# Gate and up projections of a hybrid block with the activations stationary and a few block products saved

## The chip, the cores and the metric

One core of one Trainium2 chip runs the whole kernel. The metric is the device time of one execution in microseconds (us); 0.2% of it, about 2.3 us, is the smallest difference spoken of here as a change.

## The reference

The kernel computes one block of a streaming encoder for 256 tokens of width 2048, all in fp32:

```python
h = rmsnorm(x, norm1_gain)
proj = h @ w_in                                  # attention and recurrence inputs
mixed = concat([attention(proj), recurrence(proj)])
x = x + mixed @ w_out
h2 = rmsnorm(x, norm2_gain)
ff = silu(h2 @ w_gate) * (h2 @ w_up)             # 2048 -> 5632, the part that is changed
x = x + ff @ w_down                              # 5632 -> 2048
out = rmsnorm(x, final_gain)
```

## The kernel before

Each fp32 operand of a large product is split into a high part in fp32r (ScalarE, line 86) and a low part, the difference (VectorE, line 87). A product is then three: high x high, high x low, low x high. Weights come from memory in loads of 1 MB (`load_chunk`, three buffers "raw"), all on SyncE's queue, and are split into pairs of tiles `wh` and `wl` of 1024 elements per partition, four buffers each. The eight banks of the accumulator memory are two pools of four: `pacc` ("acc") for the main sums and `paux` ("aux") for everything else.

The program has four stages. The input projection with attention and recurrence woven in comes first (to about 326 us). The `w_out` stage (to 436 us) has the activations stationary: `nat_step` (lines 142 to 144) loads 128 tokens of `ma` or `mr` as the stationary operand and streams 512 columns of `wh` or `wl`. As its columns come out they are added to `x2`, and `second_split` turns `x2` with four transposes at a time (`pair_transpose`, line 313), scales it by `norm2_gain` and splits it into `h2`, which holds the high and low parts, k-tile by k-tile, with tokens as columns.

The gate and up stage (lines 656 to 666) loops over 22 blocks of 256 columns; in each, gate and then up run through `tr_product` (lines 158 to 172). Here the weights are stationary: a tile of 128 columns of `wh` meets the high and low halves of `h2` in one product of 512 columns (line 167), and the same tile of `wl` meets the high half in one of 256 (line 169). The result comes out with the features in the partitions, which is what the down projection wants. `tr_evac` (lines 174 to 179) adds the two halves and multiplies by `R2`, a row of token scales that `row_rstd` makes by two small products (line 255); then come silu, the product, and the split into `fh` and `fl`.

The down stage works in two groups of 1024 output columns. For each pair of k-tiles a step is either plain (24 products of 512 columns, four banks c00, c01, c10, c11 by token half and column half) or fast: seven block products in place of eight, with sums of activation blocks (`row_sums`, kept in `sf`) and of weight blocks (lines 737 to 739), into c00, c01, c10 and four side banks m1, m5, m6, m7. After the last fast pair `spread` adds the side banks to `x2` (lines 774 to 782). Plain and fast pairs alternate; 7 of 22 pairs are fast in the first group and 8 in the second. The groups' last pairs run bank by bank, so that the banks are emptied one after another (`run_blocks`).

The order of the program is not the order of the engines: a list scheduler of the framework orders each engine's instructions from the dependencies, the pools' buffers and its own estimate, and each engine then works through its line in that order, waiting where it must.

Of the kernel before, what the change touches and what calls it, by code (L numbers as in the profile page):

```python
# [8 lines left out]
F32 = mybir.dt.float32  # L9
# [7 lines left out]
P = 128  # L17
# [10 lines left out]
KP = KF // 2  # L28
FAST = 8
BANKS = ("c00", "c01", "c10", "c11", "m1", "m5", "m6", "m7")  # L30
# [13 lines left out]
def hybrid_block(ctx: ExitStack, tc: tile.TileContext, x, xT, w_in, w_out, w_gu, w_down,  # L44
# [574 lines left out]
    R2 = const.tile([P, S], F32, name="R2")  # L619
    rst2 = [None]  # L620

    def second_rstd():
        s2 = small.tile([P, NT], F32, tag="ssum", name="ssum")
        nc.vector.tensor_reduce(s2, ss2, AX.X, ALU.add)
        rst2[0] = rstd_of(s2, NT, float(D), "r2")

    def second_rows():
        row_rstd(R2, rst2[0])

# [19 lines left out]
    queue.append(lambda: [f() for f in both_splits] and second_rstd())  # L649
    queue.append(second_rows)  # L650
# [5 lines left out]
    gup = tc.tile_pool(name="gup", bufs=1)  # L656
    gu = gup.__enter__()
# [8 lines left out]
    gup.__exit__(None, None, None)  # L666

    dn = ctx.enter_context(tc.tile_pool(name="dn", bufs=1))
    sf = act_t.tile([P, 2, FAST // 2, 4, 2, P], F32R, tag="hx", name="sf")
    fg = dn.tile([P, D], F32, name="fg")

    def row_sums(i):
        k4 = slice(4 * i, 4 * i + 4)
        a = dn.tile([P, 2, 2, S], F32, tag="ta", name="a")
        sm = dn.tile([P, 4, 2, P], F32, tag="tb", name="sm")
        nc.vector.tensor_tensor(a, fh[:, k4, :].rearrange("p (j k) t -> p j k t", k=2).bitcast(F32),
                                fl[:, k4, :].rearrange("p (j k) t -> p j k t", k=2).bitcast(F32), ALU.add)  # L680
# [5 lines left out]
        split(sf[:, 0, i], sf[:, 1, i], sm)  # L686

    def load_fg():
        dma(fg, fgain.to_broadcast([P, D]))
        nc.scalar.activation(warm, fg[:, 0:1], AF.Square)  # L690
        nc.scalar.activation(warm, warm, AF.Sqrt)
# [8 lines left out]
    def load_pair(g, j):  # L700
        return load_chunk(w_down, g * KP + j).rearrange("p (b n) -> p b n", n=W)

    def f_of(k, t):
        tok = slice(t * P, (t + 1) * P)
        return fh[:, k, tok], fl[:, k, tok]

    def s_of(j, i):
        return sf[:, 0, j // 2, i, j % 2, :], sf[:, 1, j // 2, i, j % 2, :]

    class Group:  # L710
        def __init__(self, g, items):
            self.g, self.items = g, items
            self.bank = {}
            ns = sum(1 for kind, _ in items if kind == "s")
            nd = len(items) - ns
            self.left = {n: 3 * (ns + 2 * nd) if n in ("c00", "c01", "c10") else
                         6 * nd if n == "c11" else 3 * ns for n in BANKS}
            self.total = dict(self.left)

        def open(self):  # L720
            for n in BANKS:
                pool, tag = (pacc, "acc") if n[0] == "c" else (paux, "aux")
                self.bank[n] = pool.tile([P, W], F32, tag=tag, name=n)

        def mul(self, n, lhs, rhs):
            if not self.bank:
                self.open()
# [5 lines left out]
        def fast(self, j):  # L733
            raw = load_pair(self.g, j)
# [9 lines left out]
            return [("m1", f_of(2 * j, 0), b11), ("m5", s_of(j, 0), t1), ("m7", s_of(j, 2), t3),  # L744
                    ("c01", s_of(j, 3), b22), ("c00", f_of(2 * j + 1, 0), b21),
                    ("m6", s_of(j, 1), t2), ("c10", f_of(2 * j + 1, 1), t4_)]

        def plain(self, j):
            raw = load_pair(self.g, j)
            steps = []  # L750
            for k in range(2):
                parts = halves_of(raw[:, 2 * k:2 * k + 2])
                steps += [(f"c{t}{h}", f_of(2 * j + k, t), parts[h if k == 0 else 1 - h])
                          for t in range(NT) for h in range(2)]
            return steps
# [5 lines left out]
        def run_blocks(self, steps, blocks, after):  # L761
            for t, h in blocks:
                self.run([st for st in steps if st[0] == f"c{t}{h}"])
                after(t, h)

# [18 lines left out]
    def add_res(gr, t, h):  # L784
        cols = gr.cols(h)
        nc.vector.tensor_tensor(x2[:, t, cols], gr.bank[f"c{t}{h}"], x2[:, t, cols], ALU.add)
        jk = dn.tile([P, W], F32, tag="jk", name="jk")
        slot = 2 * gr.g + h
        nc.scalar.activation(jk, x2[:, t, cols], AF.Square, accum_out=ss3[:, t, slot:slot + 1])

    def gained(gr, t, h):
        cols = gr.cols(h)
        nc.vector.tensor_tensor(x2[:, t, cols], x2[:, t, cols], fg[:, cols], ALU.mult)

    def finish(ps, t):
# [7 lines left out]
        jk = dn.tile([P, 2, S], F32, tag="jk", name="jk")  # L803
# [14 lines left out]
        nc.vector.scalar_tensor_tensor(x2[:, t, c0:D], x2[:, t, c0:D], r, fg[:, c0:D], ALU.mult, ALU.mult)  # L818
# [4 lines left out]
    def order_of(fast, lead):  # L823
        slow = [j for j in range(KP) if j not in fast]
        items = [("d", j) for j in slow[:lead]]
        mid = slow[lead:-2]
        for n, j in enumerate(fast):
            items += [("s", j)] + [("d", k) for k in mid[n:n + 1]]
        return items + [("d", k) for k in mid[len(fast):]] + [("d", j) for j in slow[-2:]]

    groups = [Group(0, order_of(list(range(FAST - 1)), 6))]
    todo = [(0, kind, j) for kind, j in groups[0].items]
    second = order_of(list(range(FAST)), 1)
    todo += [(1, kind, j) for kind, j in second]
    sums = list(range(FAST // 2))
    n_fast, held = [0, 0], []

    def prepare(g, kind, j):
        if g == len(groups):
            groups.append(Group(1, second))  # L840
        return groups[g].fast(j) if kind == "s" else groups[g].plain(j)

    def last_block(t, h):
        if h == 0:
            add_res(groups[1], t, h)
            gained(groups[1], t, h)
        else:
            finish(groups[1].bank[f"c{t}{h}"], t)

    edge = len(groups[0].items) - 1  # L850
    steps = prepare(*todo[0])
    for n, (g, kind, j) in enumerate(todo):
        if n == edge:
            now, steps = steps, prepare(*todo[n + 1])
            order = ((0, 0), (0, 1), (1, 0), (1, 1))
            groups[0].run_blocks(now, order, lambda t, h: add_res(groups[0], t, h))
            for t, h in order:
                gained(groups[0], t, h)
            continue
        if n < len(todo) - 2:  # L860
            groups[g].run(steps)
        else:
            held += steps
        if kind == "s":
            n_fast[g] += 1
            if n_fast[g] == sum(1 for k, _ in groups[g].items if k == "s"):
                groups[g].spread()
        if sums and n >= 1:
            row_sums(sums.pop(0))
        if n == 5:  # L870
            load_fg()
        if n + 1 < len(todo):
            steps = prepare(*todo[n + 1])
    groups[1].run_blocks(held, ((0, 0), (0, 1), (1, 0), (1, 1)), last_block)
# [8 lines left out]
def _pairs(w, c0):  # L883
    b = w[:, c0:c0 + 2 * W].reshape(KP, 2, P, 2, W)
    return [b[:, 0, :, 0], b[:, 0, :, 1], b[:, 1, :, 1], b[:, 1, :, 0]]
# [48 lines left out]
```

## Time and profile before

| | us |
|---|---|
| median of three runs (lowest, highest) | 1167.95 (1167.85, 1169.08) |
| the profiled execution | 1168.06 |
| its span, first to last instruction | 1166.2 |
| gate and up stage, in the span | 436 to 926 |
| down stage | 926 to 1152 |

The span is the part of the execution that the trace covers. PE is TensorE's products, PEld its loads of stationary operands, DVE is VectorE, ACT ScalarE. Products are pipelined: the trace gives one of 512 columns some 0.39 us from start to end, while the next one starts 0.23 us after it. So PE's pace is read from start to start, and a result is there at the end.

### The profile page before, as it was taken

Reading aid. Unit: us, or ns where it says so; the run is one execution under the profiler, and the core shown is the slowest. Engines: PE = TensorE matmul, PEld = TensorE weight load, DVE = VectorE, ACT = ScalarE, POOL = GpSimd, SP = SyncE. Lnnn points to the kernel's source line nnn. Section 1 sums busy time; section 2 is a strip of 40 time slices with the busy share of each in tenths; the row PEclk is TensorE's granted clock in tenths of the full one; section 3 lists DMA queues with packets and bytes.
Section 4 is the critical chain, followed back from the end, with each engine's and each line's share of the span. In section 5 each row is a group of like instructions: output and inputs, shape, how many; then the busy total and the mean of one; then the engine's idle time right before and its main releaser. Section 6 shows DMA issues by size and latency. Waiting matters only on the chain.

```text
span 1166.2 us, 15524 instructions
## 1 busy us (share of the span) xinstructions
PE 1154.1 (99%) x6121; PEld 989.3 (85%) x6121; DVE 815.2 (70%) x1092; ACT 624.0 (54%) x856; POOL 19.0 (2%) x33
## 2 busy tenths in 40 slices
PE   9999999999999999999999999999999999999996
PEld 7888888888888888888888888888888887888885
DVE  7577768947746556666666666666666698898885
ACT  7565556747554445444444454444454555555553
POOL 3300000000000000000000000000000000000000
PEclk9999999999999999999999999999999999999999
DMA  8655444554744555555555555555455546556561
GB/s 314 242 207 192 148 173 163 204 177 151 262 171 162 187 187 182 184 184 193 200 182 183 194 200 182 183 198 198 180 186 196 196 181 217 204 192 217 211 222 73
DMA packets 35065, 223.85 MB, mean 192 GB/s; under 512 B 4145, under 2 KB 4657, under 8 KB 9521
## 3 DMA queue, kind: packets, MB, share of 16 engines
q1 hardware_dynamic: 34992, 222.87, 54.3%
q8 instruction: 48, 0.79, 0.3%
q14 instruction: 25, 0.20, 0.1%
HBM read 220.75 MB, written 2.10 MB: 191 GB/s over the span
## 4 chain that ended last, share of the span: by engine, by line
PE 96%; DMA 1%; DVE 1%; ACT 1%; SPq 0%; issue 0%; ACTq 0%; DVEq 0%
PE acc L167 38%; PE acc L169 19%; PE c L729 15%; PE acc L142 5%; PE acc L144 5%; PE acc L143 5%; PE m L729 3%; PE vps L143 1%; PE vps L144 1%; PE vps L142 1%; DMA raw<-in_w_down_dram 1%; DMA raw<-in_w_in_dram 0%; DVE wl L87 0%; SPq L83 0%; PE pa L531 0%; PE po L550 0%
## 5 line engine op out<-in xcount | busy, mean ns | idle before, releaser
L87 DVE TENSOR_TENSOR wl<-raw,wh 128x1024 fp32r<-128x1024 f32 (+1 forms) x418 | 493.3, 1185 | 276.4 <-ACT wh L86 271.7
L86 ACT ACTIVATE wh<-raw 128x1024 fp32r<-128x1024 f32 (+1 forms) x418 | 426.2, 1023 | 367.7 <-PE acc L167 215.6
L167 PE MATMUL acc<-h,wh 128*128 128x512 f32 x1408 | 488.6, 394 | 0.0
L169 PE MATMUL acc<-h,wl 128*128 128x256 f32 x1408 | 390.9, 278 | 0.0
L167 PEld LDWEIGHTS acc<-h,wh 128*128 128x128 f32 x1408 | 264.8, 188 | 60.9
L169 PEld LDWEIGHTS acc<-h,wl 128*128 128x128 f32 x1408 | 264.4, 188 | 0.0
L167 PE MATMUL acc<-hx,wh 128*128 128x512 f32 x512 | 179.7, 395 | 0.0
L169 PE MATMUL acc<-hx,wl 128*128 128x256 f32 x512 | 143.2, 280 | 0.0
L167 PEld LDWEIGHTS acc<-hx,wh 128*128 128x128 f32 x512 | 96.2, 188 | 21.3
L729 PE MATMUL c<-wl,fh 128*128 128x512 f32 x262 | 102.2, 390 | 0.0
L729 PE MATMUL c<-wh,fh 128*128 128x512 f32 x262 | 102.0, 391 | 0.2 <-ACT wh L86 0.2
L729 PE MATMUL c<-wh,fl 128*128 128x512 f32 x262 | 102.1, 390 | 0.0
L169 PEld LDWEIGHTS acc<-hx,wl 128*128 128x128 f32 x512 | 96.7, 189 | 0.1
L177 ACT COPY tb<-acc 128x256 f32<-128x256 f32 x120 | 43.3, 364 | 78.5 <-PE acc L169 78.5
L178 DVE TENSOR_TENSOR tb<-acc,tb 128x256 f32<-128x256 f32 x120 | 50.1, 420 | 30.3 <-ACT tb L177 30.3
L729 PEld LDWEIGHTS c<-wh,fh 128*128 128x128 f32 x262 | 49.1, 188 | 11.2 <-ACT wh L86 0.6
L729 PEld LDWEIGHTS c<-wl,fh 128*128 128x128 f32 x262 | 49.2, 188 | 10.5 <-DVE wl L87 0.3
L729 PEld LDWEIGHTS c<-wh,fl 128*128 128x128 f32 x262 | 49.2, 188 | 10.1
L142 PE MATMUL acc<-wh,hx 128*128 128x512 f32 x128 | 50.5, 394 | 0.0
L144 PE MATMUL acc<-wh,hx 128*128 128x512 f32 x128 | 50.0, 390 | 0.0
L143 PE MATMUL acc<-wl,hx 128*128 128x512 f32 x128 | 49.9, 390 | 0.0
L729 PE MATMUL m<-wh,sf 128*128 128x512 f32 x90 | 32.8, 391 | 0.1
(254 smaller groups left out, 1121.6 us busy)
## 6 DMA issues: line engine op xcount, KB each, us to landing
raw<-in_w_gu_dram SPq DMA_DIRECT2D x88, 1024.0 KB, 4.8
raw<-in_w_in_dram SPq DMA_DIRECT2D x48, 1024.0 KB, 4.8
raw<-in_w_down_dram SPq DMA_DIRECT2D x44, 1024.0 KB, 4.8
raw<-in_w_out_dram SPq DMA_DIRECT2D x16, 1024.0 KB, 4.8
raw<-in_w_in_dram SPq DMA_DIRECT2D x12, 512.0 KB, 7.1
raw<-in_w_in_dram SPq DMA_DIRECT2D x8, 256.0 KB, 4.8
x<-in_x_dram SPq DMA_DIRECT2D x2, 1024.0 KB, 9.7
out_dram<-x SPq DMA_DIRECT2D x8, 256.0 KB, 2.6
```

The lines of the kernel that those rows point to most:

```text
L86: nc.scalar.activation(hi, src, AF.Copy)
L87: nc.vector.tensor_tensor(lo, src, hi.bitcast(F32), ALU.subtract)
L142: nc.tensor.matmul(ps[t], lhsT=xh[:, tok], rhs=wh, start=kt == 0, stop=False)
L143: nc.tensor.matmul(ps[t], lhsT=xh[:, tok], rhs=wl, start=False, stop=False)
L144: nc.tensor.matmul(ps[t], lhsT=xl[:, tok], rhs=wh, start=False, stop=kt == kts - 1)
L167: nc.tensor.matmul(ps[m].rearrange("p j t -> p (j t)"), lhsT=wh[:, col], rhs=both, start=kt == 0, stop=False)
L169: nc.tensor.matmul(ps[m][:, 0, :], lhsT=wl[:, col], rhs=rhs[:, kt, 0, :], start=False, stop=kt == KD - 1)
L177: nc.scalar.copy(tb, ps[m][:, 1, :])
L178: nc.vector.tensor_tensor(tb, ps[m][:, 0, :], tb, ALU.add)
L729: nc.tensor.matmul(self.bank[n], lhsT=a, rhs=b, start=self.left[n] == self.total[n], stop=self.left[n] == 1)
```

## The change

Gate and up now run in the manner of the down stage. A group is 512 gate columns beside the 512 up columns that belong to them, so there are eleven groups of eight k-tile pairs. The weights are stored in pairs of k-tiles by blocks (`_pairs`), the activations `h2` are stationary, and the weights stream by 512 columns. The class `Group` serves both projections: `Gated` and `Down` are its two kinds, and `run_groups` runs all pairs of all groups in line, with the next pair prepared behind the one that runs. The first gated group has plain pairs only; in the ten others pairs 0 and 1 are fast, in the order plain 2, fast 0, plain 3, fast 1, plain 4 to 7. `hs` holds the sums of the activation blocks of those two pairs and is made once.

The result of a group has tokens in the partitions, `ff` with one half of the tokens beside the other. The scale of a token is now one number per partition (`rst2`), applied inside silu and inside the last multiplication; `R2` and its two small products are gone. `ff_split` then turns `ff` by eight transposes into two "aux" tiles and splits these into `fh` and `fl`; this is written after the first pair of the next group. `load_fg` and its tile move into a pool that is opened later. The core of the diff:

```diff
-    for j in range(FF // S):
-        gt = gu.tile([P, 2, S], F32, tag="gt", name="gt", bufs=2)
-        tr_evac(gt, tr_product(w_gu, j * 4, h2), R2, gu)
-        nc.scalar.activation(gt, gt, AF.Silu)
-        ut = gu.tile([P, 2, S], F32, tag="ut", name="ut", bufs=1)
-        tr_evac(ut, tr_product(w_gu, j * 4 + 2, h2), R2, gu)
-        nc.vector.tensor_tensor(ut, ut, gt, ALU.mult)
-        split(fh[:, 2 * j:2 * j + 2, :], fl[:, 2 * j:2 * j + 2, :], ut)
...
+    def ff_split(ff, j):
+        for i in range(2):
+            pt = pair_transpose(lambda t: ff[:, t, :], i * 256)
+            ks = slice(4 * j + 2 * i, 4 * j + 2 * i + 2)
+            split(fh[:, ks, :], fl[:, ks, :], pt.rearrange("p j t n -> p j (t n)"))
+
+    class Gated(Group):
+        hold, ready = 1, None
+
+        def spread(self):
+            b = self.bank
+            ff = self.ff = gu.tile([P, NT, W], F32, tag="ff", name="ff")
+            u = self.u = dn.tile([P, W], F32, tag="u", name="u")
+            v = self.v = dn.tile([P, W], F32, tag="v", name="v")
+            nc.scalar.copy(ff[:, 0], b["m1"])
+            nc.vector.tensor_tensor(v, b["m6"], ff[:, 0], ALU.add)
+            nc.vector.tensor_tensor(u, b["m5"], v, ALU.add)
+            nc.vector.tensor_tensor(ff[:, 1], b["m7"], v, ALU.add)
+            nc.vector.tensor_tensor(v, b["m5"], ff[:, 1], ALU.add)
+
+        def block(self, t, h):
+            ps = self.bank[f"c{t}{h}"]
+            r = rst2[:, t:t + 1]
+            if self.ns:
+                part = (self.u, self.v)[t] if h else self.ff[:, t]
+                nc.vector.tensor_tensor(part, ps, part, ALU.add)
+                ps = part
+            elif t == 0 and h == 0:
+                self.ff = gu.tile([P, NT, W], F32, tag="ff", name="ff")
+            ff = self.ff[:, t]
+            if h == 0:
+                nc.scalar.activation(ff, ps, AF.Silu, scale=r)
+            else:
+                nc.vector.scalar_tensor_tensor(ff, ps, r, ff, ALU.mult, ALU.mult)
...
+        def between(self, n):
+            if n == 0:
+                if self.g == 0:
+                    second_end()
+                else:
+                    ff_split(gated[self.g - 1].ff, self.g - 1)
+            if n == 1 and self.g == 0:
+                row_sums(hs, h2[:, 0:2 * FASTU, 0, :], h2[:, 0:2 * FASTU, 1, :])
+
+    gated = [Gated(j, order_of(KQ, list(range(FASTU if j else 0)), 1, 1), w_gu, j * KQ, h_of, hs_of)
+             for j in range(FF // W)]
```

How the instructions move is seen at three places. The first is PE's line in the middle of the gate and up stage of before (acc is a main bank, h2 the activations):

```order
L167 MATMUL acc_4064<-h2_3174,wh_4068 128x512
L169 MATMUL acc_4064<-h2_3174,wl_4069 128x256
L167 MATMUL acc_4065<-h2_3174,wh_4068 128x512
L169 MATMUL acc_4065<-h2_3174,wl_4069 128x256
L167 MATMUL acc_4064<-h2_3174,wh_4068 128x512
L169 MATMUL acc_4064<-h2_3174,wl_4069 128x256
```

and PE's line in the changed kernel where the fast pair 0 of a group begins, behind its first plain pair (ptr are the transposed halves of the last group's ff, wh_4879 and wl_4880 the two sums of weight blocks of which m5 takes one and m7 the other, wh_4883 and wl_4884 the blocks for c01 and c00, wh_4887 and wl_4888 those for m6 and c10):

```order
L315 MATMUL ptr_4854<-ident_84,ff_4664 128x128 x4
L315 MATMUL ptr_4861<-ident_84,ff_4664 128x128 x4
L701 MATMUL m1_4891<-wh_4875,h2_3174 128x512
L701 MATMUL m1_4891<-wl_4876,h2_3174 128x512
L701 MATMUL m1_4891<-wh_4875,h2_3174 128x512
L701 MATMUL m5_4892<-wh_4879,hs_3837 128x512
...
L701 MATMUL c01_4827<-wh_4883,hs_3837 128x512
...
L701 MATMUL c00_4826<-wh_4883,h2_3174 128x512
L701 MATMUL m7_4894<-wh_4879,hs_3837 128x512
```

Where each product of 512 columns had one of 256 behind it, all are of 512 now; and m7, which the program writes right behind m5, stands four products later, behind c01 and the first of c00.

The second place is DVE's line at the same point (wl is the low part of a weight tile, ta and tb are sums of weight blocks, fl the low part of the transposed ff):

```order
L89 TENSOR_TENSOR wl_4880<-ta_4870,wh_4879 128x1024
L716 TENSOR_TENSOR ta_4952<-raw_4950 128x1024
L89 TENSOR_TENSOR wl_4884<-raw_4868,wh_4883 128x1024
L89 TENSOR_TENSOR wl_4888<-tb_4871,wh_4887 128x1024
L89 TENSOR_TENSOR fl_3830<-ptr_4854,fh_3829 128x512
L89 TENSOR_TENSOR fl_3830<-ptr_4861,fh_3829 128x512
L89 TENSOR_TENSOR wl_4919<-raw_4916,wh_4918 128x1024
```

The two steps that empty the transposed halves stand behind the last split of the fast pair, and behind the first subtraction for the next fast pair. ACT's line has the matching order, the copy wh_4887 and then the two fh.

The third place is DVE's line at the end of the group before (c00 to c11 are its main banks):

```order
L805 TENSOR_TENSOR ff_4664<-c00_4496,ff_4664 128x512
L805 TENSOR_TENSOR u_4665<-c01_4497,u_4665 128x512
L813 SCALAR_TENSOR_TENSOR ff_4664<-u_4665,rst2_3175,ff_4664 128x512
L805 TENSOR_TENSOR ff_4664<-c10_4498,ff_4664 128x512
L89 TENSOR_TENSOR wl_4876<-raw_4868,wh_4875 128x512
L805 TENSOR_TENSOR v_4666<-c11_4499,v_4666 128x512
```

The step that empties c11 has moved behind the first split of the next group's fast pair.

## Rows read from the trace of the kernel before

**Rows 1.** The page: busy us of each engine, its share of the span, instructions.

```profile
PE 1154.1 (99%) x6121; PEld 989.3 (85%) x6121; DVE 815.2 (70%) x1092; ACT 624.0 (54%) x856; POOL 19.0 (2%) x33
```

**Rows 2.** Busy time by stage: window, us, PE, PEld, DVE, ACT, POOL, clock, DMA.

```profile
326.00:436.00 110.00, 109.86 (x520) 91.34 (x519) 60.70 (x74) 57.13 (x86) 0.00 (x0) 1.00 0.50 175
436.00:926.00 490.00, 490.00 (x2831) 428.90 (x2830) 316.10 (x406) 239.83 (x316) 0.00 (x0) 1.00 0.54 190
926.00:1152.00 226.00, 225.39 (x990) 185.21 (x989) 195.21 (x219) 123.76 (x137) 0.00 (x0) 1.00 0.55 193
```

**Rows 3.** Timeline of PE (start, us, what): the gate and up stage's two ends.

```profile
436.40 0.39 PE L167 MATMUL acc<-h,wh 128*128 128x512 f32 x1
...
926.03 0.39 PE L729 MATMUL c<-wh,fh 128*128 128x512 f32 x1
```

**Rows 4.** Timeline of PE: a pair of products in that stage's middle.

```profile
599.81 0.40 PE L167 MATMUL acc<-h,wh 128*128 128x512 f32 x1
600.04 0.28 PE L169 MATMUL acc<-h,wl 128*128 128x256 f32 x1
600.16 0.39 PE L167 MATMUL acc<-h,wh 128*128 128x512 f32 x1
```

**Rows 5.** The chain of waits in order of time: start, us, what.

```profile
442.21 0.87 PE ptr L313 x8
...
448.73 0.44 PE prow L255 x4
...
1025.92 22.44 PE c L729 x99
```

**Rows 6.** Timeline of PE in the w_out stage, activations stationary.

```profile
430.51 0.39 PE L143 MATMUL acc<-wl,mr 128*128 128x512 f32 x1
430.74 0.39 PE L144 MATMUL acc<-wh,mr 128*128 128x512 f32 x1
```

**Rows 7.** Groups of instructions by shape: count, busy us, mean ns, idle before.

```profile
L87 DVE TENSOR_TENSOR wl<-raw,wh 128x1024 fp32r<-128x1024 f32 x383 | 467.8, 1225 | 268.1 <-ACT wh L86 263.4
L86 ACT ACTIVATE wh<-raw 128x1024 fp32r<-128x1024 f32 x383 | 405.0, 1059 | 357.1 <-PE acc L167 215.6 <-PE acc L144 75.3 <-PE c L729 51.5
...
L87 DVE TENSOR_TENSOR fl<-ut,fh 128x512 fp32r<-128x512 f32 x22 | 15.0, 684 | 0.0
L86 ACT ACTIVATE fh<-ut 128x512 fp32r<-128x512 f32 x22 | 13.9, 633 | 2.4 <-DVE ut L664 0.4
```

**Rows 8.** Timeline of the down stage: a release by PE, and DVE's spacing.

```profile
1045.26 0.39 PE L729 MATMUL c<-wh,fl 128*128 128x512 f32 x1
...
1045.68 1.06 ACT L86 ACTIVATE wh<-raw 128x1024 fp32r<-128x1024 f32 x1 [0.59 <-PE c L729]
...
1045.73 0.68 DVE L87 TENSOR_TENSOR wl<-raw,wh 128x512 fp32r<-128x512 f32 x1
...
1046.33 1.22 DVE L87 TENSOR_TENSOR wl<-ta,wh 128x1024 fp32r<-128x1024 f32 x1
...
1047.47 1.22 DVE L87 TENSOR_TENSOR wl<-raw,wh 128x1024 fp32r<-128x1024 f32 x1
```

**Rows 9.** Timeline of PE: a stop in the down stage and what follows it.

```profile
1014.29 0.39 PE L729 MATMUL m<-wh,sf 128*128 128x512 f32 x1
1014.93 0.50 PE L729 MATMUL m<-wl,sf 128*128 128x512 f32 x1 [0.25 <-DVE wl L87]
1015.28 0.40 PE L729 MATMUL m<-wh,sf 128*128 128x512 f32 x1
```

**Rows 10.** The page's DMA issues: KB of each, median us from issue to landing.

```profile
raw<-in_w_gu_dram SPq DMA_DIRECT2D x88, 1024.0 KB, 4.8
```

**Rows 11.** The waits: total us, times, longest.

```profile
DVE ta L737 <- DMA raw<-in_w_down_dram: 4.1, 4, 1.8
```

**Rows 12.** The chain of waits ahead of the stop of rows 9.

```profile
1005.56 6.87 DMA raw<-in_w_down_dram
...
1013.66 1.23 DVE wl L87
```

More of the change, by code (lines that the diff above doesn't have):

```diff
@@ L617, in second_split @@
                          g2[:, k:k + 1])
-    R2 = const.tile([P, S], F32, name="R2")
-    rst2 = [None]
+    rst2 = const.tile([P, NT], F32, name="rst2")
     def second_rstd():
@@ L648, in hybrid_block, with second_end @@
     queue.clear()
-    queue.append(lambda: [f() for f in both_splits] and second_rstd())
-    queue.append(second_rows)
+    def second_end():
+        for f in both_splits:
+            f()
+        second_rstd()
     ffp = ctx.enter_context(tc.tile_pool(name="ffp", bufs=1))
@@ L685, in row_sums @@
         nc.vector.tensor_tensor(sm[:, 3], a12, sm[:, 1], ALU.subtract)
[L686 to L691, printed above, removed]
+        split(dst[:, 0], dst[:, 1], sm)
     def halves_of(src):
@@ L698, in halves_of, with __init__, open @@
         return [(wh[:, i * W:(i + 1) * W], wl[:, i * W:(i + 1) * W]) for i in range(src.shape[1])]
[L700 to L708, printed above, removed]
     class Group:
-        def __init__(self, g, items):
-            self.g, self.items = g, items
+        def __init__(self, g, items, src, base, lhs, sums):
+            self.g, self.items, self.src, self.base, self.lhs, self.sums = g, items, src, base, lhs, sums
             self.bank = {}
-            ns = sum(1 for kind, _ in items if kind == "s")
+            self.ns = ns = sum(1 for kind, _ in items if kind == "s")
             nd = len(items) - ns
[L716 to L720, printed above, removed]
+            self.total = {n: 3 * (ns + 2 * nd) if n in ("c00", "c01", "c10") else
+                          6 * nd if n == "c11" else 3 * ns for n in BANKS}
+            self.left = dict(self.total)
+        def open(self, kind):
             for n in BANKS:
-                pool, tag = (pacc, "acc") if n[0] == "c" else (paux, "aux")
-                self.bank[n] = pool.tile([P, W], F32, tag=tag, name=n)
+                if n[0] == kind and self.total[n]:
+                    pool, tag = (pacc, "acc") if kind == "c" else (paux, "aux")
+                    self.bank[n] = pool.tile([P, W], F32, tag=tag, name=n)
         def mul(self, n, lhs, rhs):
-            if not self.bank:
-                self.open()
+            if n not in self.bank:
+                self.open(n[0])
             for a, b in ((lhs[0], rhs[0]), (lhs[0], rhs[1]), (lhs[1], rhs[0])):
@@ L743, in fast @@
             t2, t4_ = halves_of(tb)
[L744 to L755, printed above, removed]
+            return [("m1", self.lhs(2 * j, 0), b11), ("m5", self.sums(j, 0), t1), ("m7", self.sums(j, 2), t3),
+                    ("c01", self.sums(j, 3), b22), ("c00", self.lhs(2 * j + 1, 0), b21),
+                    ("m6", self.sums(j, 1), t2), ("c10", self.lhs(2 * j + 1, 1), t4_)]
         def run(self, steps):
@@ L759, in run, with run_blocks, order_of @@
                 self.mul(*st)
-        def run_blocks(self, steps, blocks, after):
-            for t, h in blocks:
+        def run_blocks(self, steps, after):
+            for t, h in BLOCKS:
                 self.run([st for st in steps if st[0] == f"c{t}{h}"])
                 after(t, h)
+    def order_of(pairs, fast, lead, tail):
+        slow = [j for j in range(pairs) if j not in fast]
+        items = [("d", j) for j in slow[:lead]]
+        mid = slow[lead:len(slow) - tail]
+        for n, j in enumerate(fast):
+            items += [("s", j)] + [("d", k) for k in mid[n:n + 1]]
+        return items + [("d", j) for j in mid[len(fast):] + slow[len(slow) - tail:]]
@@ new lines, in run_groups @@
+    def run_groups(groups, following=None):
+        todo = [(gr, n) for gr in groups for n in range(len(gr.items))]
+        steps, held = groups[0].ready or groups[0].prepare(*groups[0].items[0]), []
+        for i, (gr, n) in enumerate(todo):
+            ahead = None
+            if n + 1 == len(gr.items):
+                if i + 1 < len(todo):
+                    ahead = todo[i + 1][0].prepare(*todo[i + 1][0].items[0])
+                elif following is not None:
+                    following.ready = following.prepare(*following.items[0])
+                gr.run_blocks(held + steps, gr.block)
+                held = []
+                gr.end()
+            elif n + gr.hold >= len(gr.items):
+                held = held + steps
+            else:
+                gr.run(steps)
+                seen = sum(1 for kind, _ in gr.items[:n + 1] if kind == "s")
+                if gr.items[n][0] == "s" and seen == gr.ns:
+                    gr.spread()
+            gr.between(n)
+            if i + 1 < len(todo):
+                steps = ahead or todo[i + 1][0].prepare(*todo[i + 1][0].items[todo[i + 1][1]])
@@ L766, in cols @@
+    own = {}
+    class Down(Group):
+        ready = None
         def cols(self, h):
@@ L782, in spread, with block, gained, end @@
             nc.vector.tensor_tensor(x2[:, 1, c1], x2[:, 1, c1], u, ALU.add)
[L784 to L793, printed above, removed]
+        def block(self, t, h):
+            if self.g == 1 and h == 1:
+                finish(self.bank[f"c{t}{h}"], t)
+                return
+            cols = self.cols(h)
+            nc.vector.tensor_tensor(x2[:, t, cols], self.bank[f"c{t}{h}"], x2[:, t, cols], ALU.add)
+            jk = own["late"].tile([P, W], F32, tag="jk", name="jk")
+            slot = 2 * self.g + h
+            nc.scalar.activation(jk, x2[:, t, cols], AF.Square, accum_out=ss3[:, t, slot:slot + 1])
+            if self.g == 1:
+                self.gained(t, h)
+        def gained(self, t, h):
+            cols = self.cols(h)
+            nc.vector.tensor_tensor(x2[:, t, cols], x2[:, t, cols], own["fg"][:, cols], ALU.mult)
+        def end(self):
+            if self.g == 0:
+                for t, h in BLOCKS:
+                    self.gained(t, h)
+        def between(self, n):
+            if self.g == 0:
+                if n == 0:
+                    ff_split(gated[-1].ff, len(gated) - 1)
+                    gup.__exit__(None, None, None)
+                    late = ctx.enter_context(tc.tile_pool(name="late", bufs=1))
+                    own.update(late=late, fg=late.tile([P, D], F32, name="fg"))
+                elif n <= FAST // 2:
+                    ks = slice(4 * (n - 1), 4 * n)
+                    row_sums(sf[:, n - 1], fh[:, ks, :], fl[:, ks, :])
+                elif n == FAST // 2 + 1:
+                    load_fg()
     def finish(ps, t):
@@ L802, in finish @@
             nc.vector.tensor_tensor(x2[:, t, lo:hi], ps[:, lo - c0:hi - c0], x2[:, t, lo:hi], ALU.add)
-        jk = dn.tile([P, 2, S], F32, tag="jk", name="jk")
+        jk = own["late"].tile([P, 2, S], F32, tag="jk", name="jk")
         nc.scalar.activation(jk[:, 0, :], x2[:, t, c0:c1], AF.Square, accum_out=ss3[:, t, 3:4])
@@ L821, in finish @@
         dma(out[t, :, 1024:c0], x2[:, t, 1024:c0])
[L823 to L874, printed above, removed]
+    down = [Down(g, order_of(KP, list(range(FAST - 1 + g)), 1 if g else 6, 2), w_down, g * KP, f_of, s_of)
+            for g in range(2)]
+    down[0].hold, down[1].hold = 1, 2
+    run_groups(gated, down[0])
+    sf = act_t.tile([P, FAST // 2, 2, 4, 2, P], F32R, tag="hx", name="sf")
+    run_groups(down)
 def _block(w, c0, cols, kc):
```

65 lines of the change are left out of this document (45 added, 20 removed).

## Prediction

> **What bounds the kernel now.** I read the page first: TensorE (PE) is busy for 99% of the span [rows 1], and the granted clock is 1.00, the higher level of 2.4 GHz, in every stage [rows 2]. So the kernel is a queue of products, and an edit is worth what it takes out of that queue or puts into it, plus the time in which the queue stands. Then the table by stage: over the gate and up stage (436 to 926 us) PE is busy all the time, while VectorE (DVE) has 316 us of 490 and ScalarE (ACT) 240; in the down stage DVE has 195 of 226 [rows 2]. DVE and ACT are therefore cover for PE, not the bound, and the down stage matters here because it already runs the scheme that the change brings to gate and up.
>
> The stage's ends are two rows: the first gate product starts at 436.40 and the first down product at 926.03, so it lasts 489.63 us [rows 3]. Inside it a pair (512 columns of the high weights, 256 of the low ones) repeats: 599.81 to 600.04 to 600.16 [rows 4]. There are 22 x 2 x 16 x 2 = 1408 such pairs. The stage also holds one block of 8 transposes (0.87 us) and the row of scales (0.44 us) [rows 5]. So a pair costs (489.63 - 0.87 - 0.44) / 1408 = 0.3468 us.
>
> **The change, part by part.**
>
> *The form of the product.* A k-tile of one group (512 gate and 512 up columns, 256 tokens) was 8 pairs; it is now 12 products of 512 columns (2 token halves, 2 column halves, 3 products). Columns per k-tile are the same, 6144. The stage of before does not show this form with this data, but two neighbours do: 99 products of the down stage take 22.44 us, 0.2267 each [rows 5], and the w_out stage, which has the activations stationary as well, goes at 0.227 [rows 6]. Plain, the new form would be 11 x 16 x 12 = 2112 products x 0.2267 = 478.8 us against 1408 x 0.3468 = 488.3: **-9.5 us**. The ends for this price are 0.2267 and 0.2312 (the 0.3468 spread evenly over its 768 columns), which would make this term zero; I take 0.2267, since both rows with 512-column products show it.
>
> A sentence on the page: the Trainium skill, "TensorE: Matmul & The Clock Gate", section "Back-to-back issue gap", gives a gap of columns / 2.4 ns + 2.5 ns when warm, 216 ns for 512 columns, 109 for 256 and 56 for 128. Worked out from it (an estimate) the form would give 2112 x 0.2158 - 1408 x 0.325 = -1.8 us rather than -9.5, and the whole sum about -2 us, 1166. The rows differ (227 for 512, about 0.12 for 256), so the page's figures stay out of the sum.
>
> *Seven block products.* In ten of eleven groups two k-tile pairs have 21 products in place of 24: 60 products fewer, x 0.2267 = **-13.6 us**. 2052 are left.
>
> *The transposes.* Each group's gated product is now turned by 8 transposes, 11 blocks x 0.87 us [rows 5] = **+9.6 us**. They stand in PE's line, nothing hides them.
>
> *The row of scales* (two small products and their copy) goes: **-0.4 us** [rows 5]. The scale is now one number per partition.
>
> *What DVE and ACT do.* Gone are the four evacuation steps per half block and the scaling by rows; new are the block sums of the weights (1.22 + 2 x 0.68 us per fast pair), four additions after the last fast pair, six steps at a group's end and the two splits of the transposed product. With the durations of [rows 7] (steps of 1024 elements taken as wl, those of 512 as fl), a group costs DVE 6 x 2.45 + 2 x 6.9 + 2.7 + 4.1 + 1.4 = 36.8 us and ACT about 23 us, against some 43.6 us of PE (186 products x 0.2267 = 42.2, the transposes, the wait below). That is 84% for DVE; the down stage runs at 195/226 = 86% [rows 2] with PE busy. So I cost it at nothing, where PE has other work. If that cover were gone, each wl of 1.22 us too late would show on PE. The block sums of the activations (one split and five steps, about 4 us of DVE) are put by the scheduler into the w_out stage, where DVE has 60.7 us of 110 [rows 2]; nothing waits for them until the first fast pair, over 40 us on.
>
> *A wait at each group's edge.* Here the order of the changed kernel decides. All four side banks (m1, m5, m6, m7) and the two banks of the transposes share four buffers; per group six tiles go round, so m7 takes the buffer of the second transposed half, and m6 that of the first. Both are free only when DVE has written fl. In DVE's line the two fl stand behind wl<-tb of the fast pair. The walk, with T the start of the transposes: the last product of the plain pair starts at T - 0.23 and is done 0.39 later, at T + 0.16; ACT begins the copy that waits for its weights 0.03 after such an end (1045.65 to 1045.68) [rows 8], at T + 0.19, and takes 1.06: T + 1.25. DVE starts wl<-tb at T + 1.28. Behind a long step DVE starts the next after 1.14, behind a short one after 0.60 [rows 8]: first fl at T + 2.42, second at T + 3.02, done 0.68 later at T + 3.70, and m7 may start at T + 3.74. (ACT's two fh copies end before T + 2.4, so they do not hold DVE.) PE is there at T + 0.87 + 10 products x 0.2267 = T + 3.14: three of m1, three of m5, three of c01, one of c00. It stands 0.60 us. After such a stop the next product starts late too: at 1014.93, where PE had waited for wl, the following one came after 0.35 instead of 0.23 [rows 9], +0.12. So 0.72 us x 10 groups = **+7.2 us**. Its ends are nothing (if the tile takes another buffer or DVE gets there earlier) and twice that, if fl slips by another short step.
>
> *The other edge.* The next group's plain pair needs the banks of the last. The tightest is c11: its addition stands in DVE's line behind the 512-column wl of the fast pair, whose ACT copy waits for the last pair's first weights. By the same steps it is ready 1.50 us after the next group's first product, and wanted 9 products later, at 2.04: 0.54 us to spare, cost nothing. It is the next to be late.
>
> *Loads.* Still 1 MB each, 4.8 us from issue to landing [rows 10]. But a fast pair holds its load longer, and there are 20 of them here. In the down stage, of 15 fast pairs, four found DVE waiting for the load [rows 11], and one reached PE: a load that took 6.87 us and a wl that ended at 1014.89 [rows 12], so that PE's next product came 0.64 after the last instead of 0.23, with 0.12 behind it [rows 9], 0.53 us. At that rate 20 pairs cost **+0.7 us**. Before, the gate and up stage had no such wait.
>
> **Sum.** -9.5 - 13.6 + 9.6 - 0.4 + 7.2 + 0.7 = **-6.0 us**. The profiled execution took 1168.06 us (span 1166.2), 0.1 above the median of the runs, 1167.95; so 1168.06 - 6.0 = **1162.1 us**, about 0.5% faster.
>
> **The rivals.**
>
> *No wait at the edge* (chance 0.15). DVE has its wl early enough or the buffers go round otherwise: the wait is gone or under half. For it: DVE has a sixth of its time free, and the scheduler has moved m7 four products back because of this bank. Against it: the walk is made of measured steps [rows 7, 8], and wl<-tb cannot start before the weights of the plain pair are free. Time: 1162.1 - 7.2 = 1154.9, up to 1158.
>
> *Twice the wait* (0.08). If c11 loses its 0.54 us as well, or fl slips behind one more step, a group stands 1.45 us: 1169.3, no change. For it: two strict lines of steps and little room. Against it: the down stage's edge, with the same additions in it, shows no stop.
>
> *Loads late at every fast pair* (0.06), the case on the other side. There are three load buffers; a fast pair holds its own until DVE has split its last block, and the load that takes it over has to land before the subtraction at the head of its pair. It decides once loads take some 6 to 7 us instead of 4.8 [rows 10, 12]. Each then costs PE 0.53 us: 20 x 0.53 - 0.7 = +9.9, 1172.0, slower. For it: four of 15 pairs waited [rows 11]. Against it: only one of them reached PE, and the fast pairs alternate with plain ones as there.
>
> *The form gives nothing* (0.03). Products with these activations go at the old stage's pace per column, 0.2312 us: +9.5, 1171.6. The page's gap rule speaks for it, since by it both forms cost the same per column to within 0.5%; both rows of 512-column products speak against.
>
> **How the numbers follow.** The forecast case has 0.68. A difference of 0.2% (2.3 us) is about what a measurement of this kernel can tell from none. Faster by more (under 1165.6): the forecast, the first rival and a part of the second, where the wait grows by less than half, 0.68 + 0.15 + 0.02 = 0.85. Within it: 0.06, the rest of the second. Slower: 0.09, the last two. The range leaves out the two slow cases, the upper half of the second and the lowest part of the first: 1156.0 to 1167.0.
>
> **What would show it.** Right: 2052 products of 512 columns in the stage, 0.227 apart; 88 transposes of ff in blocks of 0.87; at each of ten edges one stop of 0.5 to 0.7 us on PE before the first m7, with DVE's fl as the releaser, and none at the first c11; the stage from first gate product to first down product 6 us shorter. Wrong: a stop at c11, m6 or c01, stops with a DMA behind them, a mean spacing above 0.229, or a granted clock below the higher level behind the transposes.

## The result and the profile after

| | before | after |
|---|---|---|
| median of the runs compared (lowest, highest), us | 1167.90 (1167.54, 1169.08) | 1155.77 (1155.27, 1155.93) |
| ratio, 95% interval | | 0.9894 (0.9877 to 0.9911) |
| span of the profiled execution, us | 1166.2 | 1154.1 |

The kernel is 1.1% faster, 12.1 us where 6.0 was forecast, and 0.2 us below the range (1156.0). One execution of the run without turning (1417.95 us, at a granted clock of 0.753) was a slow one and is left out of its median. The page's first line, which answers to [rows 1] (busy time, share of the span, instructions):

```profile
PE 1142.2 (99%) x5441; PEld 954.4 (83%) x5441; DVE 873.9 (76%) x1100; ACT 633.2 (55%) x819; POOL 19.0 (2%) x33
```

The table by stage, as in [rows 2] (w_out, gate and up, down; columns are busy time of PE, its weight loads, DVE, ACT, POOL, then the granted clock, DMA share and GB/s), and the rows that bound the stage, as in [rows 3]:

```profile
346.00:437.46 91.46, 91.31 (x420) 75.28 (x418) 57.13 (x75) 48.24 (x70) 0.00 (x0) 1.00 0.52 179
437.46:914.69 477.23, 477.23 (x2141) 393.53 (x2140) 374.07 (x414) 246.80 (x277) 0.00 (x0) 1.00 0.55 194
914.69:1144.73 230.04, 230.04 (x1019) 190.31 (x1018) 195.94 (x224) 127.90 (x145) 0.00 (x0) 1.00 0.54 192
```

```profile
437.46 0.39 PE L701 MATMUL c<-wh,h 128*128 128x512 f32 x1
...
914.69 0.39 PE L701 MATMUL c<-wh,fh 128*128 128x512 f32 x1
```

PE is still the bound, at the higher level of 2.4 GHz throughout. Gate and up went from 489.63 to 477.23 us: -12.4, against the forecast's -6. The down stage went from 230.96 to 230.04, although it now holds the eleventh block of transposes. Against this, the first gate product starts 1.06 us later than before. That difference is already there at 51 us, in a stage that the change leaves alone; over the nine profiles of this case that start lies between 435.8 and 437.5, with no order by kernel. So stages are compared below by their own lengths.

DVE has 374 of 477 us, 78%. The forecast's 84% was for a group with fast pairs, and by the sum of durations. From one block of transposes to the next (530.59 to 573.87) DVE's durations add up to 36.9 us, as forecast (36.8), but they overlap: it is busy for 34.80 of 43.28 us, 80%. The groups of that stretch by shape show why the PE side is as forecast (total busy, mean ns of one):

```profile
L701 PE MATMUL c<-wh,h 128*128 128x512 f32 x1168 | 366.7, 389 | 0.0
L701 PE MATMUL c<-wl,h 128*128 128x512 f32 x584 | 227.3, 389 | 0.0
L701 PE MATMUL m<-wh,hs 128*128 128x512 f32 x120 | 46.3, 400 | 0.0
...
L315 PE MATMUL ptr<-ident,ff 128*128 128x128 f32 x80 | 10.3, 272 | 0.0
```

With the five smaller groups of 512 columns the products come to the forecast 2052. What differs is the edge, the place of the term of +7.2. PE's timeline of one edge (start, duration, operation; the eight transposes start at T = 530.59):

```profile
530.36 0.40 PE L701 MATMUL c<-wh,h 128*128 128x512 f32 x1
530.59 1.03 PE L315 MATMUL ptr<-ident,ff 128*128 128x128 f32 x8
531.38 0.47 PE L701 MATMUL m<-wh,h 128*128 128x512 f32 x1
531.70 0.39 PE L701 MATMUL m<-wl,h 128*128 128x512 f32 x1
...
533.53 0.39 PE L701 MATMUL c<-wh,h 128*128 128x512 f32 x1
533.82 0.50 PE L701 MATMUL m<-wh,hs 128*128 128x512 f32 x1
534.16 0.39 PE L701 MATMUL m<-wl,hs 128*128 128x512 f32 x1
```

and ACT and DVE beside it (the view puts two fl in one line; the second fl row is the first of the two by itself, from a narrower window):

```profile
530.85 1.06 ACT L88 ACTIVATE wh<-tb 128x1024 fp32r<-128x1024 f32 x1 [1.66 <-PE c L701]
531.94 1.23 DVE L89 TENSOR_TENSOR wl<-tb,wh 128x1024 fp32r<-128x1024 f32 x1 [0.89 <-ACT wh L88]
533.08 1.28 DVE L89 TENSOR_TENSOR fl<-ptr,fh 128x512 fp32r<-128x512 f32 x2
533.08 0.68 DVE L89 TENSOR_TENSOR fl<-ptr,fh 128x512 fp32r<-128x512 f32 x1
```

Read it against the walk of the prediction. ACT starts at T + 0.26 (walk: 0.19), wl at T + 1.35 (1.28), the first fl at T + 2.49 (2.42); the second fl ends at 533.08 + 1.28 = 534.36, T + 3.77 (3.70). The walk is right to 0.07 us. But m7 starts at 533.82, half a microsecond before the second fl is done, and 0.06 after the end of the first (533.76). It waited for the other transposed half. The interval before it is 0.29 us instead of 0.23, the one behind it 0.34 (533.82 to 534.16). The waits of the stretch, where PE's engine names the same releaser (total us, times, longest):

```profile
PEld m L701 <- DVE fl L89: 3.3, 10, 0.3
```

### The profile page after: what moved, and what is told of

It is laid out like the page before. It is cut to its first block, busy times and chain, and to the rows that moved or that the text cites. A ratio compares the mean times of both kernels' runs of the same rounds, so it can differ in the third digit from the quotient of the medians.

```text
span 1154.1 us, 14105 instructions
## 1 busy us (share of the span) xinstructions
PE 1142.2 (99%) x5441; PEld 954.4 (83%) x5441; DVE 873.9 (76%) x1100; ACT 633.2 (55%) x819; POOL 19.0 (2%) x33
## 4 chain that ended last, share of the span: by engine, by line
PE 97%; DVE 1%; ACT 1%; DMA 1%; SPq 0%; issue 0%; ACTq 0%
PE c L701 51%; PE acc L169 10%; PE m L701 8%; PE acc L171 5%; PE acc L144 5%; PE acc L146 5%; PE acc L145 5%; PE ptr L315 1%; PE vps L145 1%; PE vps L146 1%; PE vps L144 1%; DMA raw<-in_w_in_dram 1%; SPq L85 0%; PE pa L533 0%; PE pa L531 0%; PE pp L346 0%
## 5 line engine op out<-in xcount | busy, mean ns | idle before, releaser
L89 DVE TENSOR_TENSOR wl<-raw,wh 128x1024 fp32r<-128x1024 f32 (+1 forms) x418 | 481.1, 1158 | 203.9 <-ACT wh L88 203.1
L88 ACT ACTIVATE wh<-raw 128x1024 fp32r<-128x1024 f32 (+1 forms) x418 | 414.7, 1003 | 355.1 <-PE c L701 217.9
L701 PE MATMUL c<-wh,h 128*128 128x512 f32 x1168 | 366.7, 389 | 0.0
L701 PEld LDWEIGHTS c<-wh,h 128*128 128x128 f32 x1168 | 219.3, 188 | 45.6
L701 PE MATMUL c<-wl,h 128*128 128x512 f32 x584 | 227.3, 389 | 0.0
L701 PEld LDWEIGHTS c<-wl,h 128*128 128x128 f32 x584 | 109.6, 188 | 22.9
L88 ACT ACTIVATE wh<-tb 128x1024 fp32r<-128x1024 f32 x35 | 37.1, 1061 | 59.2 <-PE c L701 59.2
L89 DVE TENSOR_TENSOR wl<-tb,wh 128x1024 fp32r<-128x1024 f32 x35 | 42.9, 1225 | 33.2 <-ACT wh L88 33.2
L701 PE MATMUL m<-wh,hs 128*128 128x512 f32 x120 | 46.3, 400 | 0.0
```

The lines of the kernel that those rows point to most:

```text
L88: nc.scalar.activation(hi, src, AF.Copy)
L89: nc.vector.tensor_tensor(lo, src, hi.bitcast(F32), ALU.subtract)
```

## The experiments

**Which transposed half does m7 wait for.** The four side banks and the halves get buffers by name, m7 that of the second half. PE's order is held as in the changed kernel (the lines that hold it are left out below), and it came out the same, product by product.

```diff
+    SLOT = {"m6": "x0", "m7": "x1", "m1": "x2", "m5": "x3"}
...
-                    pool, tag = (pacc, "acc") if kind == "c" else (paux, "aux")
+                    pool, tag = (pacc, "acc") if kind == "c" else (own["px"], SLOT[n])
...
-            pt = pair_transpose(lambda t: ff[:, t, :], i * 256)
+            pt = pair_transpose(lambda t: ff[:, t, :], i * 256, f"x{i}")
```

> PE's line is that of the changed kernel, product by product, but m7 gets the buffer of the second transposed half instead of the first. If the forecast's wait failed only because m7 got the half that DVE empties first, the ten stops before m7 grow from 0.07 us to about 0.65 us each, with the same 0.11 us behind them: 10 x 0.58 = 5.8 us more, 1161.6 us, about the forecast. If instead DVE reaches both halves earlier than the walk said, the stops stay under 0.2 us and the time under 1157.5 us.

Measured: 1160.71 us (1159.93 to 1161.29), ratio 0.9936 (0.9921 to 0.9951); gate and up 483.0. PE and DVE at the same edge, and the waits of the stage:

```profile
532.41 0.39 PE L712 MATMUL c<-wh,h 128*128 128x512 f32 x1
533.30 0.50 PE L712 MATMUL m<-wh,hs 128*128 128x512 f32 x1 [0.50 <-DVE fl L91]
533.64 0.39 PE L712 MATMUL m<-wl,hs 128*128 128x512 f32 x1
```

```profile
531.96 1.28 DVE L91 TENSOR_TENSOR fl<-ptr,fh 128x512 fp32r<-128x512 f32 x2
```

```profile
PEld m L712 <- DVE fl L91: 9.2, 10, 0.9
```

The second fl ends at 531.96 + 1.28 = 533.24, and m7 starts 0.06 later. The interval is 0.89 instead of 0.23, a stop of 0.66 (0.60 in the walk, whose ACT step came 0.07 too early), with 0.11 behind it. Ten edges: 483.0 - 477.2 = 5.8 us. So the step of the prediction was wrong in its buffer, not in its durations: with the buffer that it assumed, the forecast's 1162.1 would have been off by 1.4, which lies in other terms.

**The fast pairs one pair later.** Two plain pairs instead of one ahead of the first fast pair, so that the transposes, which stand behind the first pair, no longer stand directly ahead of the side banks.

```diff
-    gated = [Gated(j, order_of(KQ, list(range(FASTU if j else 0)), 1, 1), w_gu, j * KQ, h_of, hs_of)
+    gated = [Gated(j, order_of(KQ, list(range(FASTU if j else 0)), 2, 1), w_gu, j * KQ, h_of, hs_of)
```

> Two plain pairs instead of one stand ahead of the first fast pair, so the side banks are opened 5 us after the transposes. If the ten stops before m7 (0.07 and 0.11 us each) are all that is left of the wait at the edge, they go: 1.8 us less, 1154.0 us. If DVE, with the fast pairs later, is late elsewhere, the stops show before c11, c00 or m6 and the time stays at 1155.8 us or above.

Measured: 1153.14 us (1152.42 to 1153.32), ratio 0.9872 (0.9856 to 0.9889); gate and up 475.04, 2.19 shorter than after. The block and what follows it:

```profile
528.96 0.40 PE L701 MATMUL c<-wh,h 128*128 128x512 f32 x1
529.19 1.03 PE L315 MATMUL ptr<-ident,ff 128*128 128x128 f32 x8
529.99 0.47 PE L701 MATMUL c<-wh,h 128*128 128x512 f32 x1
530.30 0.39 PE L701 MATMUL c<-wl,h 128*128 128x512 f32 x1
```

No stop before a side bank is left; the next product behind the block still comes after 0.31 (530.30), so that 0.08 belongs to the block: 0.80 + 0.08, the 0.87 of [rows 5]. The edges of the changed kernel therefore cost 2.2 us, of which 10 x (0.07 + 0.11) = 1.8 is read at the stops.

**No fast pairs.** All eleven groups plain: the form of the product by itself.

```diff
-    gated = [Gated(j, order_of(KQ, list(range(FASTU if j else 0)), 1, 1), w_gu, j * KQ, h_of, hs_of)
+    gated = [Gated(j, order_of(KQ, list(range(0)), 1, 1), w_gu, j * KQ, h_of, hs_of)
```

> All pairs of gate and up plain, the rest as changed. By the terms of the sum: 60 products more at 0.227 us are 13.6 us, the ten stops go for 1.8 us: 1167.6 us, no change against the kernel before, that is, the new form of the product pays for the transposes and no more. If the form gave nothing, 1177 us; if it gave more than 9.5 us, under 1166 us.

Measured: 1165.88 us (1165.67 to 1167.13), ratio 0.9986 (0.9977 to 0.9995). The gate and up stage of its table:

```profile
435.90:924.54 488.64, 488.64 (x2202) 405.65 (x2200) 248.06 (x235) 214.22 (x228) 0.00 (x0) 1.00 0.54 190
```

It has no stop, so 2112 products and eleven blocks of 0.877 (ten of ff, and the one of x2 that before has too) fill it: (488.64 - 9.65) / 2112 = 0.2268 each. The form is worth 479.0 - 488.3 = -9.3 us (forecast -9.5). And 488.64 - 475.04 = 13.6 us is what the 60 products come to, where neither kernel has a stop at an edge: exactly their term. The down stage is 230.04 here too. The time came 1.7 us below the expected 1167.6, on the side where the form would be worth more than 9.5; the stage says 9.3. Most of what is missing lies ahead of the stage, which starts at 435.90 in this profile and at 437.46 in the one after.

**No turning.** The transposes are left out, and the copies read ff as it stands; the down projection then works on data that are not turned.

```diff
-            pt = pair_transpose(lambda t: ff[:, t, :], i * 256)
+            pt = ff[:, i, :].rearrange("p (j n) -> p j n", n=S)
...
```

> The eleven blocks of eight transposes are left out and fh and fl are filled from the gated product as it stands, so the down projection works on unturned data. If the transposes stand in PE's line in full, 11 x 0.88 = 9.7 us go, and with them the ten stops, 1.8 us: 1144.3 us. If a part of them was hidden behind waits that come back now, the time is above 1147 us.

Measured: 1143.81 us (1142.75 to 1144.14), ratio 0.979 (0.9773 to 0.9806), 12.0 us below the changed kernel, where eleven blocks at 0.87 (9.6) and the 2.2 of the edges come to 11.8. By stage it is less tidy. Down is 0.85 shorter, one block. Gate and up is 10.1 shorter where ten blocks and ten edges come to 10.9, and it starts 0.8 us earlier in this profile (436.69). One group lost 1.0 us at 820 us, to DVE's v and ff (0.8 in stops, 0.2 behind them). In that group alone DVE had waited for a load, for the first fast pair of the next group, and the additions behind it in DVE's line came late:

```profile
812.35 1.23 DVE L716 TENSOR_TENSOR ta<-raw 128x1024 f32<-128x1024 f32 x1 [2.30 <-DMA raw<-in_w_gu_dram]
```

**A third fast pair.** Its sums of activations are kept in the unwritten end of fh and fl. This asks what the forecast cost at nothing: DVE's work.

```diff
+FASTX = 3
...
+    hx2 = [f_[:, 40:44, :].rearrange("p a (b n) -> p a b n", n=P) for f_ in (fh, fl)]
...
+            if n == 2 and self.g == 0:
+                row_sums(hx2, h2[:, 4:8, 0, :], h2[:, 4:8, 1, :])
...
-    gated = [Gated(j, order_of(KQ, list(range(FASTU if j else 0)), 1, 1), w_gu, j * KQ, h_of, hs_of)
+    gated = [Gated(j, order_of(KQ, list(range(FASTX if j else 0)), 1, 1), w_gu, j * KQ, h_of, hs_of)
```

> A third k-tile pair of each of the ten groups in the form of seven products (its activation sums are kept in the unwritten tail of fh and fl): 30 products fewer, x 0.2268 = -6.8 us on PE, and 4.45 us more of DVE in a group, 41.2 of some 42.4. Theory (DVE is cover as long as its sum for a group lies under PE's): 1155.8 - 6.8 = 1149.0 us, gate and up 470.4, stops at the edges as in the changed kernel. Rival (the order of DVE's steps counts, not their sum: with 97% of DVE's time spoken for, one wl of a fast pair comes 1.2 us late in each group): 1149.0 + 10 x 0.4 or more, 1153 us or above, with new stops that DVE ends.

Measured: 1149.27 us (1147.77 to 1149.91), ratio 0.9841 (0.9825 to 0.9858), the lowest median of all and ahead of both kernels. Its gate and up stage:

```profile
437.27:907.55 470.28, 470.28 (x2112) 387.89 (x2111) 409.89 (x464) 263.51 (x298) 0.00 (x0) 1.00 0.57 197
```

470.28 against 470.4 expected, the same ten small stops and no new ones. DVE is at 87% of the stage, PE at 100%. The first group, with plain pairs only, lowers that share: in a group with fast pairs (529.69 to 572.27) DVE is busy for 38.42 of 42.58 us, 90%. The sum by single durations, 97%, had been too high: the durations of DVE's steps overlap (a step of 1.22 us has the next behind it after 1.14 [rows 8]), and busy time counts the overlap once.

**Four fast pairs.** As above with FASTX = 4.

> Four fast pairs a group, every second k-tile pair: 60 products fewer than the changed kernel, -13.6 us on PE, but DVE's steps by their durations come to 45.7 us a group against 41.8 of PE. Theory (DVE's sum decides): DVE cannot keep up, PE stands in every group behind DVE steps, and the time stays above that of three pairs, between 1150 and 1160 us (it was DVE's free sixth that made two pairs free). Rival (DVE overlaps enough of its steps, and PE stays the bound): 1155.8 - 13.6 = 1142.2 us without new stops.

Measured: 1153.02 us (1152.52 to 1153.68), ratio 0.9875 (0.986 to 0.9889); gate and up 474.62. The time is where the theory had put it:

```profile
436.22:910.84 474.62, 468.59 (x2082) 380.69 (x2080) 444.67 (x508) 278.53 (x318) 0.00 (x0) 1.00 0.56 194
```

Over the stage DVE has 30 us free (444.67 of 474.62), but 19 of them lie in the first group, which has plain pairs only. The first group, and then one with fast pairs, from one block of transposes to the next:

```profile
436.22:486.07 49.85, 49.85 (x225) 41.34 (x224) 31.11 (x38) 25.34 (x31) 0.00 (x0) 1.00 0.52 179
529.03:571.86 42.83, 42.34 (x189) 34.41 (x188) 42.13 (x49) 25.55 (x30) 0.00 (x0) 1.00 0.57 196
```

There DVE is busy for 42.13 of 42.83 us, 98%, while PE without stops would need 41.7 (180 products at 0.2268 and a block of 0.87). So the theory's reason holds as well: DVE cannot keep up. PE stands at two fixed places of every group (duration; in brackets the idle time and what ended it):

```profile
518.72 0.19 PEld L702 LDWEIGHTS c<-wl,h 128*128 128x128 f32 x1 [0.54 <-DVE wl L90]
...
522.72 0.39 PE L702 MATMUL c<-wh,h 128*128 128x512 f32 x1
...
523.48 0.47 PE L702 MATMUL c<-wh,h 128*128 128x512 f32 x1 [0.38 <-DVE ff L807]
```

The first is a wl that comes late in the plain pair behind the fourth fast one, 0.28 us. The second is the next group's first product, which comes 0.76 after the last one instead of 0.23: it waits for the addition that empties its bank of the group before. With 0.1 behind each, over ten groups, and with a few stops at m7, that makes some 12 us; 474.6 - 12 = 462.6, against 475.04 - 13.6 = 461.4 for a stage without stops (1.2 is not placed). In this order the third and the fourth fast pair follow each other, and one plain pair is left behind them; another order was not tried. With DVE's 42.1 us in a group against the 42.6 that a group takes with three pairs, an estimate leaves it some 0.5 us a group at best.

**Three fast pairs, begun one pair later.** Both edits: FASTX = 3, and 2, 1 in the order. The transposes stay behind the first pair, as in the run with the lead alone; it is the fast pairs that move.

> The third fast pair together with the transposes one pair later in the stream (lead 2), which had closed the stops at the edges and was worth 2.2 us of the stage by itself. Theory (the two gains stand in different places of PE's line and add): 1149.0 - 2.4 = 1146.6 us, the stage 468.2, no stop over 0.05 at the edges. Rival (DVE has no room left, so the split of the transposed product that lead 2 moves behind more of DVE's steps comes late): no better than three pairs with the lead of one, 1149 or above, with stops that DVE's fl ends.

Measured: 1150.42 us (1150.2 to 1150.85), ratio 0.9852 (0.9838 to 0.9867): no better than three pairs alone. The rival holds in its time, not in its step (an addition, not fl) and not in its reason, as DVE's load shows below. The stage, then PE and DVE at a group's end:

```profile
436.55:909.19 472.64, 470.66 (x2111) 387.75 (x2110) 405.91 (x459) 263.13 (x298) 0.00 (x0) 1.00 0.56 195
```

```profile
523.13 0.39 PE L702 MATMUL c<-wh,h 128*128 128x512 f32 x1
523.71 0.47 PE L702 MATMUL c<-wh,h 128*128 128x512 f32 x1 [0.18 <-DVE ff L807]
524.01 0.39 PE L702 MATMUL c<-wl,h 128*128 128x512 f32 x1
```

```profile
519.95 0.68 DVE L798 TENSOR_TENSOR u<-m,v 128x512 f32<-128x512 f32 x1
520.55 0.68 DVE L799 TENSOR_TENSOR ff<-m,v 128x512 f32<-128x512 f32 x1
521.15 1.22 DVE L90 TENSOR_TENSOR wl<-raw,wh 128x1024 fp32r<-128x1024 f32 x1
522.28 0.68 DVE L800 TENSOR_TENSOR v<-m,ff 128x512 f32<-128x512 f32 x1
522.88 0.68 DVE L807 TENSOR_TENSOR ff<-c,ff 128x512 f32<-128x512 f32 x1
```

The stops at m7 are gone, as in the run with the lead alone. But only one plain pair is left behind the last fast one, so the four steps that spread the side banks still stand in DVE's line when the group ends. The addition to the first bank runs to 522.88 + 0.68 = 523.56, and the next group's first product, due at 523.36, starts at 523.71, with 0.08 behind it: 0.43 an edge. Ten of them are the difference between 472.64 and the 468.2 expected. Three pairs with a lead of one have the same work, DVE at 90% of a group against 89% here (38.24 of 42.81 us, 529.24 to 572.05), and no such stop. So this edge is not a matter of DVE's load: it is the place of its steps that stops PE.

## Why the prediction was right or wrong

The profile's account by stages, each term measured where a run isolates it:

| term | forecast | measured |
|---|---|---|
| form of the product | -9.5 | -9.3 |
| 60 products fewer | -13.6 | -13.6 |
| eleven blocks of transposes | +9.6 | +9.6 |
| row of scales | -0.4 | not isolated |
| wait at each group's edge | +7.2 | +2.2 |
| loads | +0.7 | 0 in gate and up |
| the down stage beside its block | no term | -1.8 |

**The step that failed** is "m7 takes the buffer of the second transposed half". m7 took the buffer of the first: it starts 0.06 us after the first fl, and in the run where it was given the second half's buffer it starts 0.06 after the second. The first fl frees its tile 0.60 us earlier, which is the 0.60 of the stop. I had counted six tiles round four buffers in the order in which a group opens them (m1, m5, m6, m7). But m7 is used ahead of m6, in the program and in PE's line alike, and it was m7, used first, that got the buffer freed first. That the order of use decides is read from this edge alone; no run changed it by itself. The term was 5.0 too large, and the first rival, "No wait at the edge", had named this ("the buffers go round otherwise") with a chance of 0.15 and 1154.9 to 1158 us. 1155.8 lies in it; my range, from 1156.0, cut off its lowest part. With this term right the forecast would have been 1157.1, inside the range: that the time fell below it is owed to two smaller misses as well, the loads and the down stage.

**Loads.** That 20 fast pairs would find their loads late at the rate of the down stage of before was wrong too: the waits of gate and up hold no DMA at all. With a third fast pair DVE did wait for loads there, 12 times and 4.6 us in all, and no stop of PE came of it.

**The down stage** became 1.8 us shorter beside its additional block, for which the forecast had no term. Before, PE lost 1.7 us there that it did not lose after, at three places, and only the last of them, 0.53 us, had a load at its head [rows 9, 12]. The first, 0.22 us, was a wait for the old gate and up stage's evacuation (`tr_evac`), which the change removes. The second, 0.92 us with its tails, stood in the first fast pair, where ACT's copy had waited for DVE:

```profile
928.88 0.19 PEld L729 LDWEIGHTS c<-wh,fh 128*128 128x128 f32 x1 [0.36 <-DVE tb L178]
...
961.52 1.06 ACT L86 ACTIVATE wh<-tb 128x1024 fp32r<-128x1024 f32 x1 [2.76 <-DVE tb L739]
962.64 0.19 PEld L729 LDWEIGHTS m<-wh,sf 128*128 128x128 f32 x1 [0.57 <-ACT wh L86]
```

DVE went without a pause there, with the sums of activation blocks for the down stage among the steps of its first fast pair; they were done only 31.8 us into the stage (957.80), and 25.6 us into it after the change (940.25). Its waits on loads, as in [rows 11], after and in the run without fast pairs:

```profile
DVE ta L716 <- DMA raw<-in_w_down_dram: 0.8, 1, 0.8
```

```profile
DVE ta L716 <- DMA raw<-in_w_down_dram: 0.5, 2, 0.4
```

Instead of four waits of 4.1 us in all. The run without fast pairs has the same stretch of 230.04, so the fast pairs of gate and up are not the reason. What moved those sums and the loads was not tried, and before was profiled once: this stays open.

**The sum.** -9.3 - 13.6 + 9.6 - 0.4 + 2.2 - 1.8 = -13.3 us; the two spans differ by 12.1. The rest is the later start of the stage in this one profile (+1.06) and 0.2 at its end. The median also moved by 12.1; whether the changed kernel starts the stage later on the whole, nine single profiles don't settle.

**What held.** The price of the form: the rows with 512-column products in the stages nearby gave 0.2267, the stage has 0.2268. The Trainium skill, "TensorE: Matmul & The Clock Gate", section "Back-to-back issue gap", would have made of this term -1.8 us, by an estimate, with its 216 ns for 512 columns. It gives them for a product by itself, and about 131 ns for a stream of weight loads and products. The run without fast pairs has 227 ns, so the trace agrees with neither figure. By its -9.3 us the rival "The form gives nothing" falls. The transposes at 0.87 a block, in line and with nothing to hide them, held; so did the granted clock of 1.00 behind them. DVE as cover at no cost held, and with a third pair's work as well; with a fourth it did not. "Twice the wait" did not come, and the c11 edge, "the next to be late", cost nothing; with the last fast pair moved towards the group's end, it was the addition of the first bank there that became late, by 0.35 us. "Loads late at every fast pair" is excluded by the waits.

## What to carry to other kernels

Before you price a wait for a buffer, follow the buffer in the order in which its tiles are used, not in the order in which the program opens them: which tile it takes over, and which step frees that tile. Here the durations of the walk were right to 0.07 us, and the one wrong name was worth 5 us. Read a helper engine's share in the group that repeats, not over the stage. At 90% of a group it cost nothing here, at 89% four microseconds in ten groups, and at 98% it set the pace. Short of that, what decided in these runs is how many of its steps stood between the last fast pair and the edge where the bound engine needs a buffer: with two plain pairs behind the last fast one there was no stop at that edge, with one there was.

## What the runs showed of the hardware

A stop on PE has a tail whose size hardly depends on the stop: behind the stop of 0.07 us the next product came 0.11 late (534.16 after 533.82), behind that of 0.66 also 0.11 (533.64 after 533.30), behind that of 0.35 with both edits 0.08 (524.01 after 523.71). Behind a block of transposes it is 0.08. The granted clock was 1.00 in the w_out, gate and up and down stages of every profile, also in the run with ten stops of 0.66 us.
